# One decoder block on one core: token rows added in single steps between the last two experts' own operations, float32 spread of the last results, one root chain

## The chip, the cores and the metric

The kernel runs on one core of one Trainium2 chip. The metric is device time in microseconds (us) of one execution. A core has five engines with queues of their own that run in order and wait for each other through semaphores: PE (TensorE, matmuls; PEld is its weight loads), DVE (VectorE), ACT (ScalarE), POOL (GpSimd) and SP (SyncE, which here only issues DMAs).

## The reference, cut to what matters

512 tokens of width 1024. A token mixer comes first, then a mixture of 16 experts (4 groups of 4) of which each token takes two of one group, then a last norm.

```python
h = h + gate_m * _hybrid_mixer(...)
xf = _rms_norm(h, norm_ffn_w[l]) * (1.0 + scale_f) + shift_f
# in _hierarchical_moe, for each group gi:
    hg = jnp.einsum('td,edf->tef', xf, w_gate[gi])
    hu = jnp.einsum('td,edf->tef', xf, w_up[gi])
    act = jax.nn.silu(hg) * hu * comb[:, gi, :, None]
    out = out + jnp.einsum('tef,efd->td', act, w_down[gi])
h = h + gate_f * _hierarchical_moe(...)
return _rms_norm(h, norm_out_w)
```

## The kernel before

The kernel gathers each expert's tokens into a block of 128 rows, so that each of the 16 experts costs one pass of gate and up (`gate_up`: two sums of 24 matmuls of 128x512), SiLU and multiplication (L1497 on ACT, L1498 on DVE), transposes of the hidden rows with their split into a rounded and a residual part (`h_prep`, L1503 to L1506), and down (`down`: two halves `q` of 12 matmuls). Matmuls run on fp32r operands; float32 precision comes from three passes over a high and a low part (`PASSES`).

Experts 0 to 13 write their rows, by token and choice, to a DRAM buffer `yg`. The last two (14 and 15, `e >= NY`) don't: their results, times a weight per slot (`wsl`) and the gate row, are evicted to `ys` (L1520) and spread to the tokens by matmuls with a 0/1 selector `selT` (`spread_parts` makes the two parts, `spread_rows` issues the matmuls).

Meanwhile the rows of `yg` are read back, one DMA for each of the four token tiles t (`y_rows`), and added to the residual stream `hbs[t]` with each token's weights `comb` and the gate row (`add_rows`: a scaling on ACT, then three steps of 128x1024: one multiply-add on DVE, a multiplication and an addition on DVE, for tile 3 on POOL). At the end each half tile gets the spread sum from PSUM (L1754), is squared and summed on ACT (L1756), and for tiles 0 and 1 multiplied by the output norm's weights on POOL (L1758). `root` makes 1/rms for two tiles by a chain of 13 tiny DVE instructions (L1749, then `rsqrt`, L171 to L179), and the tiles are scaled (L1765 on ACT, L1767 on DVE) and stored (L1768).

The engines run what the program issues in its order. `after(j)` is called between the parts of `gate_up` and issues work of other kinds there; what it issues stands in the queues of ACT and DVE ahead of the SiLU and of L1498, since these are issued after the last matmul of `gate_up`.

Of the kernel before, what the change touches and what calls it, by code (L numbers as in the profile page):

```python
# [10 lines left out]
F32 = mybir.dt.float32  # L11
FR = mybir.dt.float32r
I32 = mybir.dt.int32
AF = mybir.ActivationFunctionType
ALU = mybir.AluOpType
# [4 lines left out]
D = 1024  # L20
S = 512
NT = S // P
# [4 lines left out]
EPS = 1e-6  # L27
# [87 lines left out]
def body(ctx, tc, x, c, mod_w, mod_b, norm_mix_w, w_in, gdn_conv_w, gdn_a_log, gdn_dt_bias, gdn_norm_w, w_out,  # L115
         norm_ffn_w, w_group, b_group, w_router, b_router, w_gate, w_up, w_down, norm_out_w, c_sq, c_ret, c_rt, out):
    nc = tc.nc
    act, dve, pe, pool, sp = nc.scalar, nc.vector, nc.tensor, nc.gpsimd, nc.sync
# [24 lines left out]
    rl_free, hi_free, lo_free = [], [], []  # L143
# [108 lines left out]
    def flat(t, n):  # L252
        return t.rearrange("p (k n) -> p k n", n=n)
# [44 lines left out]
    def two(key, n):  # L298
        return [flat(t, n) for t in parts[key]]
# [737 lines left out]
    for b, (kind, c0) in enumerate(wblocks):  # L1037
# [3 lines left out]
        if kind == "G":  # L1041
            pt = ps_m.tile([P, 512], F32, tag="m", name="pm")
            for k in range(KB):
                for i, (w, a) in enumerate(PASSES):
                    pe.matmul(pt[:8], lhsT=ws[w][:, k, :8], rhs=xs[a][k // 4][:, k % 4],
                              start=(k == 0 and i == 0), stop=(k == KB - 1 and i == 2))
# [109 lines left out]
    comb = cp.tile([P, NT, 2], F32, name="comb")  # L1156
# [147 lines left out]
    for t in range(NT):  # L1304
        py = [pst("py") for _ in range(2)]
        for q in range(4):
            w2 = two(("o", q), 256)
            for k in range(KB):
                for i, (a, w) in enumerate(PASSES):
                    pe.matmul(py[q // 2][:, (q % 2) * 256:(q % 2 + 1) * 256], lhsT=mhl[t][a][:, k], rhs=w2[w][:, k],  # L1310
                              start=(k == 0 and i == 0), stop=(k == KB - 1 and i == 2))
# [151 lines left out]
    def halves(t):  # L1463
        return t[:, 0:4], t[:, 4:8]
# [35 lines left out]
    def h_prep(hh, al=fresh):  # L1500
        th, tl, pt = al("th"), al("tl"), al("ht")
        for k in range(4):
            pe.transpose(out=pt[:, k * P:(k + 1) * P], in_=hh[:, k * P:(k + 1) * P], identity=ident)  # L1503
        p3 = pt.rearrange("p (k q) -> p k q", k=4)
        act.copy(out=th, in_=p3)  # L1505
        dve.tensor_tensor(out=tl, in0=p3, in1=th.bitcast(F32), op=ALU.subtract)  # L1506
        return th, tl

    def down(e, tt, q, o, al=fresh, wt=None):
        pt = al(f"py{q}")  # L1510
        hi_lo = two((e, 4 + q), 512)
        for k in range(4):
            for i, (a, w) in enumerate(PASSES):
                pe.matmul(pt, lhsT=tt[a][:, k], rhs=hi_lo[w][:, k],  # L1514
                          start=(k == 0 and i == 0), stop=(k == 3 and i == 2))
        if e == "ov" or e < NY:
            return lambda: act.copy(out=o, in_=pt)
        g = flat(loaded["g", 0], D)[:, 0, q * 512:(q + 1) * 512]
        if wt is not None:
            return lambda: dve.scalar_tensor_tensor(out=o, in0=pt, scalar=wt, in1=g, op0=ALU.mult, op1=ALU.mult)  # L1520
        return lambda: dve.tensor_tensor(out=o, in0=pt, in1=g, op=ALU.mult)
# [79 lines left out]
    tts, yb, spread, hbs = {}, {}, {}, {}  # L1601
# [12 lines left out]
        act.copy(out=selT[j], in_=pt.rearrange("p (t q) -> p t q", t=NT))  # L1614
        dve.tensor_copy(out=wsl[:, j:j + 1], in_=pw[:, :1])

    def spread_parts(j, ys, qq=(0, 1)):

        t = spread[j] if j in spread else flat(hi_free.pop(0), D)
        for q in qq:  # L1620
            qs = slice(q * 512, (q + 1) * 512)
            act.copy(out=t[:, 0, qs], in_=ys[:, qs])
            dve.tensor_tensor(out=t[:, 1, qs], in0=ys[:, qs], in1=t[:, 0, qs].bitcast(F32), op=ALU.subtract)
        spread[j] = t

    def spread_rows(j, t, q, pt):
        for a in range(2):
            pe.matmul(pt, lhsT=selT[j][:, t], rhs=spread[j][:, a, q * 512:(q + 1) * 512],
                      start=(j == 0 and a == 0), stop=(j == 1 and a == 1))

    def y_rows(t):

        if not rl_free:
            more_raw(slot_of[id(hi_free.pop(0))])
        yb[t] = flat(rl_free.pop(0), D)
        sp.dma_start(out=yb[t], in_=yg[2 * t * P:2 * (t + 1) * P].rearrange("(p i) d -> p i d", i=2))

    def add_rows(t):

        y0, y1 = (yb[t][:, i] for i in range(2))  # L1640
        act.activation(out=y0, in_=y0, func=AF.Copy, scale=comb[:, t, 0:1])
        dve.scalar_tensor_tensor(out=y0, in0=y1, scalar=comb[:, t, 1:2], in1=y0, op0=ALU.mult, op1=ALU.add)
        eng = pool if t == 3 else dve
        eng.tensor_tensor(out=y0, in0=y0, in1=gn[:, 0], op=ALU.mult)  # L1644
        eng.tensor_tensor(out=hbs[t], in0=hbs[t], in1=y0, op=ALU.add)  # L1645


    selT = []
    ws_gen = []
    for e in range(NE):  # L1650
        last = e == NE - 1
        hh = fresh("hh")

        def after(j, e=e):
            release((e, j))
            if j < (3 if e != EC else 0):
                split_next()
            for _ in range(2):
                if ws_gen and next(ws_gen[0], "end") == "end":
                    ws_gen.pop(0)  # L1660
            if e == 0 and j == 0:
                slot_rows()
                x_load(toks[:, 8:9], X)
            if e == 1 and j == 0:
                more_blocks()
            if e == NE - 1 and j < 2:
                last_slots(j)
            if e == NE - 1 and j >= 2:
                y_rows(j - 1)
                add_rows(j - 2)  # L1670
        if e == 0:
            xx1 = x_first(1)
            split_next(2)
        if last:
            assert pos[0] == len(seq)
            gn = flat(loaded["g", 0], D)
            for i in range(2):
                for j in range(2):
                    hbs[2 * i + j] = flat(loaded["t", i], D)[:, j]
            y_rows(0)  # L1680
        reserve[0] = 4 if e == EC - 1 else 0
        gate_up(e, xx, hh, after)
        if e == EC:
            more()
            split_next(4)
        elif not last:
            split_next()
        if e == NY:
            for j in range(2):
                for t in range(NT):  # L1690
                    dve.tensor_scalar(out=slot_sel(j)[:, t], in0=iota, scalar1=posa[:, t, NY + j:NY + j + 1],  # L1691
                                      scalar2=M[:, t, NY + j:NY + j + 1], op0=ALU.is_equal, op1=ALU.mult)
        if e == 0:
            xx = xx1
        elif not last:
            xx = x_prep(X)
            if e + 2 < NE:
                x_load(toks[:, (e + 2) * 4:(e + 2) * 4 + 1], X)
            if e == 1:
                rl_free.append(em.tile([P, 2048], F32, tag="rawl", name="rawl"))  # L1700
                load()
        if e:
            ys = fresh("ys")
            w = wsl[:, e - 1 - NY:e - NY] if e - 1 >= NY else None
            down(e - 1, tts[e - 1], 0, ys[:, :512], wt=w)()
            release((e - 1, 4))
            if not last:
                split_next()
        tts[e] = h_prep(hh)
        if e == 2:  # L1710
            ws_gen += [w012, w3]
        if e:
            down(e - 1, tts[e - 1], 1, ys[:, 512:], wt=w)()
            release((e - 1, 5))
            if w is None:
                y_store(rows[:, (e - 1) * 4:(e - 1) * 4 + 1], ys)
            else:
                spread_parts(0, ys)
                y_rows(3)
            if not last:  # L1720
                split_next()
        if e == NY:
            selT += halves(em.tile([P, KB, P], FR, tag="X", name="selT"))


    e = NE - 1
    ys = fresh("ys")
    ev = [down(e, tts[e], q, ys[:, q * 512:(q + 1) * 512], wt=wsl[:, 1:2]) for q in range(2)]
    pf = {}
    tq = [(t, q) for t in range(NT) for q in range(2)]  # L1730
    add_rows(2)
    for t, q in tq[:6]:
        pf[t, q] = list(banks.values())[2 * t + q]
        spread_rows(0, t, q, pf[t, q])
    for q in range(2):
        ev[q]()
        spread_parts(1, ys, (q,))
    add_rows(3)
    for t, q in tq:
        if t == NT - 1:  # L1740
            pf[t, q] = ps_m.tile([P, 512], F32, tag="m", name="pf")
            spread_rows(0, t, q, pf[t, q])
        spread_rows(1, t, q, pf[t, q])
    fs = em.tile([P, 2 * NT], F32, name="fs")
    fr = em.tile([P, NT], F32, name="fr")
    def root(t0):
        f2 = fs[:, 2 * t0:2 * t0 + 4].rearrange("p (t q) -> p t q", q=2)
        r2 = fr[:, t0:t0 + 2]
        dve.tensor_tensor(out=r2, in0=f2[:, :, 0], in1=f2[:, :, 1], op=ALU.add)  # L1749
        rsqrt(r2, r2, 1.0 / D, EPS)  # L1750

    for t, q in tq:
        h = hbs[t][:, q * 512:(q + 1) * 512]
        dve.tensor_tensor(out=h, in0=h, in1=pf[t, q], op=ALU.add)  # L1754
        j = em.tile([P, 512], F32, tag="hh", name="junk", bufs=2)
        act.activation(out=j, in_=h, func=AF.Square, accum_out=fs[:, 2 * t + q:2 * t + q + 1])  # L1756
        if t < 2:
            pool.tensor_tensor(out=h, in0=h, in1=gn[:, 1, q * 512:(q + 1) * 512], op=ALU.mult)  # L1758
        if (t, q) == (NT - 1, 0):
            root(0)  # L1760
    root(2)
    for t in range(NT):
        h = hbs[t]
        if t < 2:
# [33 lines left out]
```

## Time and profile before

| | us |
|---|---|
| median of 3 runs | 1088.85 |
| lowest, highest | 1085.78, 1088.94 |
| profiled execution, its own time | 1089.13 |
| its span (first to last instruction) | 1087.3 |

| engine | busy us | share of the span |
|---|---|---|
| PE | 963.2 | 89% |
| PE weight load | 835.7 | 77% |
| DVE | 736.0 | 68% |
| ACT | 518.0 | 48% |
| POOL | 295.7 | 27% |

The mean granted TensorE clock is 0.94 of 2.4 GHz. The shares are means over the whole span; the change touches only its last 65 us or so. Times in the rows below are counted from the start of the span.

### The profile page before, as it was taken

Reading aid. Unit: us, or ns where it says so; the run is one execution under the profiler, and the core shown is the slowest. Engines: PE = TensorE matmul, PEld = TensorE weight load, DVE = VectorE, ACT = ScalarE, POOL = GpSimd, SP = SyncE. Lnnn points to the kernel's source line nnn. Section 1 sums busy time; section 2 is a strip of 40 time slices with the busy share of each in tenths; the row PEclk is TensorE's granted clock in tenths of the full one; section 3 lists DMA queues with packets and bytes.
Section 4 is the critical chain, followed back from the end, with each engine's and each line's share of the span. In section 5 each row is a group of like instructions: output and inputs, shape, how many; then the busy total and the mean of one; then the engine's idle time right before and its main releaser. Section 6 shows DMA issues by size and latency. Waiting matters only on the chain. (4 is left out here: it accounts for less than half of the span.)

```text
span 1087.3 us, 14839 instructions
## 1 busy us (share of the span) xinstructions
PE 963.2 (89%) x5672; PEld 835.7 (77%) x5672; DVE 736.0 (68%) x1167; ACT 518.0 (48%) x750; POOL 295.7 (27%) x281
## 2 busy tenths in 40 slices
PE   4899989989889999999999977599967899999972
PEld 2579957768799999999989975478846688888851
DVE  3478246767886652566448594699766789898966
ACT  4453134433342331362233333478655778888823
POOL 2018733553447645000000154111100111111103
PEclk8999998989989989999999988799988999999987
DMA  9857742232345532232157245789784799999941
GB/s 297 268 177 249 222 138 83 83 113 82 128 136 145 165 117 79 69 107 79 40 161 252 98 154 75 283 322 388 245 307 171 287 389 384 376 383 365 358 164 78
DMA packets 139538, 217.91 MB, mean 200 GB/s; under 512 B 14942, under 2 KB 72830, under 8 KB 138692
## 3 DMA queue, kind: packets, MB, share of 16 engines
q1 hardware_dynamic: 124640, 182.45, 48.9%
q0 software_dynamic: 11296, 30.66, 9.1%
q10 hardware_dynamic: 3524, 3.78, 1.0%
q8 instruction: 47, 0.77, 0.3%
q14 instruction: 31, 0.25, 0.1%
HBM read 204.98 MB, written 21.16 MB: 208 GB/s over the span
## 5 line engine op out<-in xcount | busy, mean ns | idle before, releaser
L294 DVE TENSOR_TENSOR lo<-raw,hi 128x1024 fp32r<-128x1024 f32 (+1 forms) x194 | 242.0, 1287 | 57.9 <-ACT hi L293 57.8
L293 ACT CAST hi<-raw 128x1024 fp32r<-128x1024 f32 (+1 forms) x198 | 197.4, 1043 | 28.1 <-PE gu L1492 21.6
L1064 PE MATMUL pm<-lo,xh 128*128 128x256 f32 x640 | 186.5, 291 | 11.5 <-DVE ty L650 7.1
L1064 PE MATMUL pm<-hi,xh 128*128 128x256 f32 x640 | 186.5, 291 | 0.0
L1064 PE MATMUL pm<-hi,xl 128*128 128x256 f32 x640 | 185.9, 290 | 0.0
L1064 PEld LDWEIGHTS pm<-lo,xh 128*128 128x128 f32 x640 | 125.8, 196 | 12.4 <-issue 7.2
L1064 PEld LDWEIGHTS pm<-hi,xh 128*128 128x128 f32 x640 | 125.9, 197 | 0.5
L1064 PEld LDWEIGHTS pm<-hi,xl 128*128 128x128 f32 x640 | 125.8, 197 | 0.3
L1492 PE MATMUL gu<-lo,xth 128*128 128x512 f32 x256 | 103.7, 405 | 10.7 <-DVE lo L1559 9.2
L1492 PE MATMUL gu<-hi,xtl 128*128 128x512 f32 x256 | 103.1, 403 | 2.0 <-DVE xtl L1460 2.0
L1492 PE MATMUL gu<-hi,xth 128*128 128x512 f32 x256 | 103.1, 403 | 0.0
L393 POOL TENSOR_TENSOR rawm<-rawm 128x512 f32<-128x512 f32 (+2 forms) x96 | 100.3, 1044 | 7.7
L493 POOL DMA_DIRECT2D rawm<-in_mod_w_dram x32 | 29.7, 927 | 213.8 <-PE modp L510 202.3
L1064 PE MATMUL pm<-xl,hi 128*128 128x512 f32 x168 | 70.1, 417 | 2.0 <-ACT hi L293 1.6
L1064 PE MATMUL pm<-xh,lo 128*128 128x512 f32 x168 | 71.1, 423 | 0.5 <-DVE lo L294 0.5
L1064 PE MATMUL pm<-xh,hi 128*128 128x512 f32 x168 | 70.9, 422 | 0.0
L1492 PEld LDWEIGHTS gu<-lo,xth 128*128 128x128 f32 x256 | 49.4, 193 | 23.4 <-DVE lo L1559 9.6
L1008 ACT ACTIVATE sg<-pm 128x512 f32<-128x512 f32 x32 | 18.9, 597 | 95.9 <-PE pm L1064 81.1
L1514 PE MATMUL py<-lo,th 128*128 128x512 f32 x144 | 61.8, 429 | 1.4 <-ACT th L1505 1.4
L391 POOL TENSOR_TENSOR rawm<-rawm,cs 128x1024 f32<-128x1024 f32 x32 | 61.4, 1918 | 0.6
L1451 POOL DMA_INDIRECT X<-xfd,toks x14 | 20.3, 1448 | 148.8 <-PE xe L1472 128.8
L1492 PEld LDWEIGHTS gu<-hi,xtl 128*128 128x128 f32 x256 | 49.2, 192 | 14.3 <-DVE xtl L1460 2.4
(405 smaller groups left out, 2037.0 us busy)
## 6 DMA issues: line engine op xcount, KB each, us to landing
raw<-in_w_in_dram SPq DMA_DIRECT2D x32, 1024.0 KB
raw<-in_w_up_dram SPq DMA_DIRECT2D x26, 1024.0 KB
raw<-in_w_gate_dram SPq DMA_DIRECT2D x24, 1024.0 KB
raw<-in_w_down_dram SPq DMA_DIRECT2D x20, 1024.0 KB
rawm<-in_mod_w_dram POOLq DMA_DIRECT2D x32, 512.0 KB, 5.2
rawe<-in_w_down_dram SPq DMA_DIRECT2D x9, 1024.0 KB
rawe<-in_w_up_dram SPq DMA_DIRECT2D x8, 1024.0 KB
mod<-in_mod_w_dram SPq DMA_DIRECT2D x7, 1024.0 KB
```

What stands on the lines that cost most here:

```text
L293: act.copy(out=hi, in_=rw)
L294: (eng or dve).tensor_tensor(out=lo, in0=rw, in1=hi.bitcast(F32), op=ALU.subtract)
L391: pool.tensor_tensor(out=r, in0=r, in1=cs.unsqueeze(2).to_broadcast([P, KB, n]), op=ALU.mult)
L393: pool.tensor_tensor(out=r[:, :m], in0=r[:, :m], in1=r[:, m:2 * m], op=ALU.add)
L493: pool.dma_start(out=r, in_=mw[:, :, (16 + i) * P:(17 + i) * P])
L1008: act.activation(out=sg, in_=pt, func=AF.Sigmoid)
L1064: pe.matmul(o, lhsT=l, rhs=r, start=st, stop=sp__)
L1451: pool.indirect_dma_start(out=X, out_offset=None, in_=xfd, in_offset=bass.IndirectOffsetOnAxis(ap=at, axis=0), bounds_check=S - 1, oob_is_ ...
L1492: pe.matmul(pt, lhsT=xx[a][k // 4][:, k % 4], rhs=hi_lo[w][:, k % 4], start=(k == 0 and i == 0), stop=(k == KB - 1 and i == 2))
L1514: pe.matmul(pt, lhsT=tt[a][:, k], rhs=hi_lo[w][:, k], start=(k == 0 and i == 0), stop=(k == 3 and i == 2))
```

## The change

Four edits, all at the end of the program.

1. `add_rows` becomes a generator that yields after each of its three DVE steps, all tiles' on DVE; its scaling on ACT is a function of its own (`scale_rows`). Nothing of it is issued inside `gate_up` any more. Tile 0's steps are issued one or two at a time between the operations of experts 14 and 15, tile 1's after expert 14's spread parts, tiles 2 and 3's after expert 15's evictions.
2. Tile 3's multiplication and addition move from POOL to DVE.
3. Expert 15's results are spread by one float32 matmul from `ys` for each tile and half (L1762 of the changed program), in place of two fp32r matmuls of its two parts, which are no longer made.
4. One root chain for all four tiles stands behind the last addition, in place of one for tiles 0 and 1 (ahead of the last addition) and one for 2 and 3.

```diff
-    def spread_parts(j, ys, qq=(0, 1)):
+    def spread_parts(j, ys):
...
+    def scale_rows(t):
+        y0 = yb[t][:, 0]
+        act.activation(out=y0, in_=y0, func=AF.Copy, scale=comb[:, t, 0:1])
+
     def add_rows(t):
 
         y0, y1 = (yb[t][:, i] for i in range(2))
-        act.activation(out=y0, in_=y0, func=AF.Copy, scale=comb[:, t, 0:1])
         dve.scalar_tensor_tensor(out=y0, in0=y1, scalar=comb[:, t, 1:2], in1=y0, op0=ALU.mult, op1=ALU.add)
-        eng = pool if t == 3 else dve
-        eng.tensor_tensor(out=y0, in0=y0, in1=gn[:, 0], op=ALU.mult)
-        eng.tensor_tensor(out=hbs[t], in0=hbs[t], in1=y0, op=ALU.add)
+        yield
+        dve.tensor_tensor(out=y0, in0=y0, in1=gn[:, 0], op=ALU.mult)
+        yield
+        dve.tensor_tensor(out=hbs[t], in0=hbs[t], in1=y0, op=ALU.add)
+        yield
+
+    def all_rows(ts):
+        for t in ts:
+            yield from add_rows(t)
...
                 y_rows(j - 1)
-                add_rows(j - 2)
...
-            down(e - 1, tts[e - 1], 0, ys[:, :512], wt=w)()
+            ev = down(e - 1, tts[e - 1], 0, ys[:, :512], wt=w)
+            if last:
+                scale_rows(0)
+                adds = all_rows(range(NT))
+                next(adds)
+                next(adds)
+            ev()
...
         tts[e] = h_prep(hh)
+        if last:
+            next(adds)
...
                 spread_parts(0, ys)
                 y_rows(3)
+                for t in range(1, NT):
+                    scale_rows(t)
+                for _ in range(3):
+                    next(adds)
...
-    add_rows(2)
     for t, q in tq[:6]:
         pf[t, q] = list(banks.values())[2 * t + q]
         spread_rows(0, t, q, pf[t, q])
     for q in range(2):
         ev[q]()
-        spread_parts(1, ys, (q,))
-    add_rows(3)
+    for _ in adds:
+        pass
     for t, q in tq:
...
-        spread_rows(1, t, q, pf[t, q])
+        pe.matmul(pf[t, q], lhsT=selT[1][:, t].bitcast(F32), rhs=ys[:, q * 512:(q + 1) * 512], start=False, stop=True)
...
-        if (t, q) == (NT - 1, 0):
-            root(0)
-    root(2)
+    f2 = fs.rearrange("p (t q) -> p t q", q=2)
+    dve.tensor_tensor(out=fr, in0=f2[:, :, 0], in1=f2[:, :, 1], op=ALU.add)
+    rsqrt(fr, fr, 1.0 / D, EPS)
```

What the diff alone doesn't tell is the order on the engines. DVE, behind the last copy of the slot weights (`wsl`), as it was (`raw_88`, `rawe_5906` hold the rows of tiles 0 and 1, `raw_4775` the residual stream of both):

```order
L1615 COPY wsl<-py_9060 128x1
L1642 SCALAR_TENSOR_TENSOR raw_88<-raw_88,comb 128x1024
L1644 TENSOR_TENSOR raw_88<-raw_88,raw_89 128x1024
L1645 TENSOR_TENSOR raw_4775<-raw_4775,raw_88 128x1024
L1642 SCALAR_TENSOR_TENSOR rawe_5906<-rawe_5906,comb 128x1024
L1644 TENSOR_TENSOR rawe_5906<-rawe_5906,raw_89 128x1024
L1645 TENSOR_TENSOR raw_4775<-raw_4775,rawe_5906 128x1024
L1498 TENSOR_TENSOR hh<-hh,gu_5885 128x512
L1520 SCALAR_TENSOR_TENSOR ys<-py_9108,wsl,raw_89 128x512
L1506 TENSOR_TENSOR tl<-xe,th 128x512
```

And now, from the same place to the second eviction of the last expert:

```order
L1498 TENSOR_TENSOR hh<-hh,gu_5885 128x512
L1645 SCALAR_TENSOR_TENSOR raw_88<-raw_88,comb 128x1024
L1647 TENSOR_TENSOR raw_88<-raw_88,raw_89 128x1024
L1520 SCALAR_TENSOR_TENSOR ys<-py_9100,wsl,raw_89 128x512
L1506 TENSOR_TENSOR tl<-xe,th 128x512
L1649 TENSOR_TENSOR raw_4775<-raw_4775,raw_88 128x1024
L1520 SCALAR_TENSOR_TENSOR ys<-py_9126,wsl,raw_89 128x512
L1623 TENSOR_TENSOR hi_5459<-ys,hi_5459 128x512 x2
L1645 SCALAR_TENSOR_TENSOR rawe_5906<-rawe_5906,comb 128x1024
L1647 TENSOR_TENSOR rawe_5906<-rawe_5906,raw_89 128x1024
L1649 TENSOR_TENSOR raw_4775<-raw_4775,rawe_5906 128x1024
L1520 SCALAR_TENSOR_TENSOR ys<-py_9152,wsl,raw_89 128x512
```

L1498 has moved ahead of all adding steps; tile 0's steps (L1645, L1647, L1649) stand apart, around the eviction and `tl`.

ACT, behind the second selector cast (`selT`) and up to the squares, as it was:

```order
L1614 CAST selT<-xe 128x512
L1641 ACTIVATE raw_88<-raw_88,comb 128x1024
L1641 ACTIVATE rawe_5906<-rawe_5906,comb 128x1024
L1497 ACTIVATE hh<-gu_5884 128x512
L1505 CAST th<-xe 128x512
L1622 CAST hi_5459<-ys 128x512 x2
L1641 ACTIVATE rawe_5907<-rawe_5907,comb 128x1024
L1622 CAST hi_92<-ys 128x512 x2
L1641 ACTIVATE raw_5037<-raw_5037,comb 128x1024
```

And now:

```order
L1614 CAST selT<-xe 128x512
L1497 ACTIVATE hh<-gu_5884 128x512
L1640 ACTIVATE raw_88<-raw_88,comb 128x1024
L1505 CAST th<-xe 128x512
L1622 CAST hi_5459<-ys 128x512 x2
L1640 ACTIVATE rawe_5906<-rawe_5906,comb 128x1024
L1640 ACTIVATE rawe_5907<-rawe_5907,comb 128x1024
L1640 ACTIVATE raw_5037<-raw_5037,comb 128x1024
```

The SiLU (L1497) has moved ahead of the scalings, the other three scalings stand together, and two casts are gone.

PE, the difference behind the last expert's down (`hi_5459` holds expert 14's parts, `hi_92` held expert 15's):

```order
 L1628 MATMUL xe<-hi_5459,selT 128x512 x8
-L1628 MATMUL gu_5884<-hi_92,selT 128x512 x2
-L1628 MATMUL gu_5885<-hi_92,selT 128x512 x2
-L1628 MATMUL xe<-hi_92,selT 128x512 x8
+L1762 MATMUL gu_5884<-ys,selT 128x512
+L1762 MATMUL gu_5885<-ys,selT 128x512
+L1762 MATMUL xe<-ys,selT 128x512 x4
 L1628 MATMUL pf<-hi_5459,selT 128x512 x2
-L1628 MATMUL pf<-hi_92,selT 128x512 x2
+L1762 MATMUL pf<-ys,selT 128x512
```

One float32 matmul stands where two fp32r ones stood.

## Rows read from the trace of the kernel before

**Rows 1.** Who waited for whom, 1034 to the end: total us, times, longest.

```profile
PE xe L1503 <- DVE hh L1498: 8.1, 1, 8.1
```

**Rows 2.** Order of time (ACT, PE, DVE): start, us, instruction, [idle before, releaser].

```profile
1031.88 0.58 ACT L1614 CAST selT<-xe 128x512 fp32r<-128x512 f32 x1
...
1039.35 1.15 ACT L1641 ACTIVATE raw<-raw,comb 128x1024 f32<-128x1024 f32 x1 [6.88 <-DMA raw<-yg]
...
1040.23 0.39 PE L1514 MATMUL py<-hi,tl 128*128 128x512 f32 x1
1040.54 1.28 DVE L1642 SCALAR_TENSOR_TENSOR raw<-raw,comb 128x1024 f32<-128x1024 f32 x1 [6.48 <-ACT raw L1641]
...
1042.89 0.58 ACT L1497 ACTIVATE hh<-gu 128x512 f32<-128x512 f32 x1
...
1047.97 0.68 DVE L1498 TENSOR_TENSOR hh<-hh,gu 128x512 f32<-128x512 f32 x1
1048.57 0.74 DVE L1520 SCALAR_TENSOR_TENSOR ys<-py,wsl,raw 128x512 f32<-128x512 f32 x1
```

**Rows 3.** By stretch: length, busy (count) of five engines, clock, DMA share, GB/s.

```profile
1044.00:1052.00 8.00, 3.29 (x11) 2.83 (x12) 5.93 (x7) 1.10 (x2) 0.00 (x0) 0.57 0.17 70
...
22.30:24.30 2.00, 1.98 (x3) 0.50 (x3) 0.00 (x0) 0.00 (x0) 0.00 (x0) 0.50 1.09 341
```

**Rows 4.** Order of time, PE: matmuls behind the hole, and of the spread.

```profile
1050.05 0.63 PE L1514 MATMUL py<-hi,th 128*128 128x512 f32 x1
...
1050.47 0.63 PE L1514 MATMUL py<-hi,tl 128*128 128x512 f32 x1
...
1059.85 2.03 PE L1628 MATMUL xe<-hi,selT 128*128 128x512 f32 x8
```

**Rows 5.** Order of time, POOL and DVE, from 1065 to the last multiplications.

```profile
1065.63 2.41 POOL L1644 TENSOR_TENSOR raw<-raw,raw 128x1024 f32<-128x1024 f32 x1 [38.26 <-DVE raw L1642]
...
1070.43 4.93 POOL L1758 TENSOR_TENSOR raw<-raw,raw 128x512 f32<-128x512 f32 x4
1070.50 0.69 DVE L1754 TENSOR_TENSOR raw<-raw,pf 128x512 f32<-128x512 f32 x1 [1.37 <-POOL raw L1645]
1071.11 0.60 DVE L1749 TENSOR_TENSOR fr<-fs 128x2 f32<-128x2 f32 x1
...
1071.75 1.20 DVE L171 TENSOR_SCALAR nx<-fr 128x2 f32<-128x2 f32 x1
...
1077.06 0.68 DVE L1754 TENSOR_TENSOR raw<-raw,pf 128x512 f32<-128x512 f32 x1
...
1078.59 0.16 DVE L1749 TENSOR_TENSOR fr<-fs 128x2 f32<-128x2 f32 x1 [0.85 <-ACT junk L1756]
...
1081.16 2.48 DVE L1767 SCALAR_TENSOR_TENSOR raw<-raw,fr,raw 128x1024 f32<-128x1024 f32 x2
```

**Rows 6.** Order of time, DVE and ACT: spread parts, then half-tile additions.

```profile
1054.19 1.46 DVE L1623 TENSOR_TENSOR hi<-ys,hi 128x512 fp32r<-128x512 f32 x2
...
1060.51 0.62 ACT L1622 CAST hi<-ys 128x512 fp32r<-128x512 f32 x1 [4.53 <-DVE ys L1520]
...
1066.66 2.48 DVE L1754 TENSOR_TENSOR raw<-raw,xe 128x512 f32<-128x512 f32 x4
```

**Rows 7.** Order of time, PE, early: float32 matmuls of 128x512 (two instructions each).

```profile
22.32 2.05 PE L336 MATMUL rrow<-diag,ones 128*128 128x512 f32 x2 [6.80 <-DVE diag L334]
...
258.59 1.02 PE L570 MATMUL rs<-rqk 128*128 128x512 f32 x2
...
259.68 0.39 PE L1064 MATMUL pm<-xl,hi 128*128 128x512 f32 x1
```

**Rows 8.** Order of time, ACT and SP's queue: last scalings, first store.

```profile
1078.46 2.17 ACT L1765 ACTIVATE raw<-raw,fr 128x1024 f32<-128x1024 f32 x2
...
1079.62 4.38 SPq L1768 DMA_DIRECT2D out_dram<-raw  x4
```

**Rows 9.** By stretch, columns as in rows 3: the stores.

```profile
1080.40:1085.90 5.50, 0.00 (x0) 0.00 (x0) 3.10 (x6) 0.23 (x1) 0.00 (x0) 0.50 0.96 381
```

More of the change, by code (lines that the diff above doesn't have):

```diff
@@ L1615, in last_slots @@
         dve.tensor_copy(out=wsl[:, j:j + 1], in_=pw[:, :1])
-    def spread_parts(j, ys, qq=(0, 1)):
-        t = spread[j] if j in spread else flat(hi_free.pop(0), D)
-        for q in qq:
+    def spread_parts(j, ys):
+        t = flat(hi_free.pop(0), D)
+        for q in range(2):
             qs = slice(q * 512, (q + 1) * 512)
@@ L1628, in spread_rows @@
             pe.matmul(pt, lhsT=selT[j][:, t], rhs=spread[j][:, a, q * 512:(q + 1) * 512],
-                      start=(j == 0 and a == 0), stop=(j == 1 and a == 1))
+                      start=(a == 0), stop=False)
     def y_rows(t):
@@ L1742, in body @@
             spread_rows(0, t, q, pf[t, q])
-        spread_rows(1, t, q, pf[t, q])
+        pe.matmul(pf[t, q], lhsT=selT[1][:, t].bitcast(F32), rhs=ys[:, q * 512:(q + 1) * 512], start=False, stop=True)
     fs = em.tile([P, 2 * NT], F32, name="fs")
     fr = em.tile([P, NT], F32, name="fr")
[L1746 to L1750, printed above, removed]
     for t, q in tq:
```

## Prediction

> **What bounds the kernel now.** The front of the kernel isn't touched, so I read only the end: from the last expert's gate and up products, at about 1024 us, to the end of the span at 1087.3. I began with the waits of this stretch, then the order of time on ACT, DVE and PE, then the chain that ended last.
>
> The longest wait on PE is 8.1 us: the transposes of the last expert's hidden rows wait for the multiplication `hh` on DVE [rows 1]. The order of time says why [rows 2]. ACT ends its selector cast at 1032.46 and then stands in the scaling of token tile 0's rows until 1039.35, when those rows land. The SiLU is queued behind that scaling and tile 1's and runs at 1042.89, although its gate sums were done before the selector cast. DVE does the six adding steps of tiles 0 and 1 from 1040.54 to 1047.97 and only then `hh`. PE's last matmul before the hole starts at 1040.23. Behind the hole its granted clock averages 0.57 over 1044 to 1052, that is 1.2 GHz for most of it [rows 3], and matmuls start 0.42 us apart [rows 4], where 0.234 is the distance at 2.4 GHz (eight in 2.03 us, the last 0.39 long).
>
> The second hole is on DVE at the very end. POOL does two of tile 3's steps from 1065.63, both about 2.4 us, and its four weight multiplications wait until 1070.43. DVE stands until 1070.50 for tile 3's sum, adds one half tile, and then does the first root chain while POOL multiplies: its first instruction takes 0.60 us instead of 0.16, the next three 1.20 each instead of 0.17 (the second chain, 13 instructions from 1078.59 to 1081.16, shows the undisturbed size). The last half tile is added only at 1077.06, the second chain lasts to 1081.16, and two multiplications (2.48) and the stores end the span [rows 5].
>
> **The change, step by step.** I lay DVE's new queue out from 1040.54, the start of tile 0's first adding step. That start stays: it hangs on rows landing at 1039.35 plus a scaling, and neither their issue nor what is ahead of it moves. What changes ahead of it: the SiLU now follows the selector cast (about 1032.5) and `hh` follows the last up matmul. PE issues 12 matmuls between the last up matmul and 1040.23 + 0.234, so `hh` runs near 1038 and is done when PE comes to the transposes at 1040.5. The hole of 8.1 us goes, and with it the half clock.
>
> Prices from the rows: a tile's three steps take 7.43/2 = 3.72 us, an eviction 0.74, a residual 0.73 (two in 1.46), the hi cast on ACT 0.62, a scaling 1.15 [rows 2, 6].
> - Tile 0's steps one and two end at 1043.1. First half of the eviction to 1043.8, the residual `tl` of the hidden rows to 1044.5, step three (1.2) to 1045.7, second half evicted at 1046.45, its hi cast on ACT to 1047.1, its residual to 1047.85.
> - ACT's scaling of tile 1 stands behind that cast: to 1048.3. This costs DVE 0.4 us, the only wait that I find on it. Tile 1's steps to 1052.0, the last expert's two evictions to 1053.5.
> - Tiles 2 and 3, both now on DVE: 7.43, to 1060.9. The moved part is POOL's two passes of 2.4 us, which cost DVE 2.4 in all; what goes against it are two casts, two residuals (1.46) and the handing to and fro between them.
> - Eight half-tile additions, 0.6 apart (four in 2.48, the last 0.68 long) [rows 5, 6]: the last starts at 1060.9 + 7 x 0.6 = 1065.1. Before, it started at 1077.06, so 12 us have gone by here.
>
> PE beside this: after the transposes (to about 1040.9) twelve matmuls to 1043.9, then the last expert's 24. The third of them needs `tl` (1044.5), so they end near 1050. Twelve spread matmuls end at 1052.5 and the eight float32 ones start with the first evicted half at 1052.8. For their price the trace has one case at the full clock: a 128x512 float32 matmul is two instructions, and from its start to the next but one matmul lie 259.68 - 258.59 = 1.09 us, less 0.234 for the matmul between: 0.86 [rows 7]. The other end is 2.05 us, early in the kernel at a granted clock of 0.50 [rows 3, 7]. I take 0.86, since PE has no hole ahead of it. Eight of them and the four remaining spread matmuls are 6.9 + 0.9, to 1060.6, and each is there before DVE asks for it; the last with 4.5 us to spare. That cover hides the 3.1 us that eight at 0.86 cost over the sixteen at 0.234 removed; it is gone from 0.86 + 4.5/8 = 1.4 us each, and from there each 0.1 us more costs 0.8.
>
> The one root chain starts 1.53 us after the last addition (1077.06 to 1078.59, with the square between): 1066.6. POOL's first multiplication follows the first addition and its square, some 1.4 us, so 1062.3, and four take 4.93: to 1067.2. So the chain's first instruction meets the fourth multiplication and waits for its end, 0.6 us; the rest runs free, 2.4 us (the whole chain took 2.57), to 1069.65. In the rows of before one DVE instruction ended with each POOL instruction, which is how I price this. The Trainium skill (SBUF — State Buffer, section "SBUF: two separate sides") states such a rule: DVE and POOL share a pair of ports that one of them holds for a whole instruction, while the other blocks. It speaks against a single chain placed behind POOL's work, and the 1.20 us rows agree with it; by the rule as by the row it costs 0.6 here, or more if POOL is later (a rival below).
>
> Now the stores. Tiles 0 and 1 used to be scaled and stored while the second chain ran: first store issued at 1079.62. Now all four wait for one chain. The first is ready after a scaling of 1.13 (two took 2.17, overlapping a little) at 1070.8, the others by 1072.2 [rows 8]. In before 2.10 MB moved in the 5.5 us from 1080.4 at a DMA share of 0.96, beginning 0.8 after the first issue, and the span ended 1.4 later [rows 9]. At a share of one that is 5.3: 1070.8 + 0.8 + 5.3 + 1.4 = 1078.3. By the other bound, the last multiplication, it would be 1072.15 plus the 3.66 that lay between its end and the span's end before (1083.64 to 1087.3): 1075.8. I take the later, since the transfers kept nearly all the DMA busy.
>
> **The sum.** 1087.3 - 1078.3 = 9.0 us less. The profiled execution took 1089.13, 1.83 over its span and 0.28 over the median of 1088.85. So 1080.1 against that execution, and 1079.9 by the median. The first hole gives back about 8, the second about 4 more with the root; the queue of stores takes some 2.5 of it.
>
> **Rivals.**
> - Stores don't bind, because the DMA engines take the four together faster than one by one: 1075.8 + 1.83 - 0.28 = 1077.3. For it: some of the 5.5 us were gaps between issues. Against: the share of 0.96. Chance 0.12.
> - POOL holds the whole head of the chain as before, if its multiplications start about 3 us later than I have them. The first chain of before, 1071.11 to 1077.0, was 5.9 against 2.57, so 3.4 more instead of my 0.6: 1079.9 + 2.8 = 1082.7. For it: exactly these rows. Against: POOL has nothing else in its queue now. Chance 0.12.
> - No change: the rows of tile 0 now stand on DVE ahead of `tl` and of both evictions, so each us that they land after 1039.35 moves PE and everything behind by one. From 5.7 us late on, what is left is within 3.3 us (0.3%) of before, about what a measurement can tell. For it: DVE takes its instructions in order, and the landing already ended ACT's 6.88 us wait. Against: nothing ahead of these transfers changes. Chance 0.05.
> - Slower: PE stays at the half clock from the transposes on, and the float32 matmuls take the 2.05 of that row. Then 36 matmuls at 0.42 end at 1056.7, the twelve spread ones at 1061.8, and 8 x 2.05 + 4 x 0.42 end at 1079.9. With 1.53, the chain's 2.57, 1.13 and 7.5 for the stores the span is 1092.6, the time 1094.1. At the full clock it would take 3.0 us for each float32 matmul to become slower by 0.3%. For it: the half clock was there in this very stretch. Against: the hole that came before it is gone, and the granted clock was back at 2.4 GHz, by the 0.234, once PE worked again. Chance 0.03.
> - The rest, 0.02, I leave to sides that I don't see.
>
> **The numbers.** The forecast has 0.66, with a range of its own of 1078.5 to 1082: the handovers between ACT and DVE may each cost some tenths more, and the runs of before lie 3 us apart. The range given reaches to both neighbours, 1075.5 to 1084, and leaves out the two far cases. Faster by over 0.3%: forecast and both neighbours, 0.90; within 0.3%: 0.06; slower: 0.04.
>
> **What would show it.** `hh` near 1038 and no wait of PE's transposes for it; PE's clock at 1.00 until the float32 matmuls end; these 0.86 us apart, done near 1061; no POOL instruction before the multiplications; the first half-tile addition near 1061 and eight without a gap; the root's first instruction stretched, the others at 0.17; the four stores issued within 1.5 us and the DMA full behind them. I am wrong if DVE waits anywhere for PE between 1048 and 1065, if tile 0's rows land later, or if the chain's head shows 1.2 us instructions again.

## The result and the profile after

The changed kernel takes 1076.32 us (median of 4 runs, 1073.98 to 1081.39) against 1088.89 (4 runs, 1085.78 to 1089.45): a ratio of 0.9897, 95% interval 0.9855 to 0.9938. It is faster, by 11.2 us of the 1088.89, between 6.8 and 15.8 (the medians alone lie 12.6 apart). Its profiled execution took 1077.67, with a span of 1075.9.

The end of the program is compared best from one instruction that every version has: the first adding step of tile 0 on DVE (1040.54 before, 1038.45 after). From it to the end of the span I call "the stretch" below: 46.8 us before, 37.45 after, 9.3 less.

PE's wait for `hh` [rows 1] is gone. These are the waits of 1034 to 1080 after (engine, instruction, releaser: total us, times, longest). POOL and ACT stand long for work that isn't due yet; DVE, whose queue sets this stretch, has waits of 4.6 and 0.8 ahead of its first step, of 0.4 and 0.9 behind it, and no more:

```profile
ACT raw L1640 <- DMA raw<-yg: 5.2, 1, 5.2
DVE hh L1498 <- PE gu L1492: 4.6, 1, 4.6
...
DVE fr L1773 <- ACT junk L1769: 0.9, 1, 0.9
DVE raw L1645 <- ACT raw L1640: 0.8, 1, 0.8
...
DVE rawe L1645 <- ACT rawe L1640: 0.4, 1, 0.4
```

The order of time after (start, us, instruction, [idle before, releaser]), the part that answers to [rows 2], [rows 5] and [rows 8]:

```profile
1037.01 0.69 DVE L1498 TENSOR_TENSOR hh<-hh,gu 128x512 f32<-128x512 f32 x1 [4.62 <-PE gu L1492]
...
1037.26 1.15 ACT L1640 ACTIVATE raw<-raw,comb 128x1024 f32<-128x1024 f32 x1 [5.22 <-DMA raw<-yg]
...
1038.45 1.28 DVE L1645 SCALAR_TENSOR_TENSOR raw<-raw,comb 128x1024 f32<-128x1024 f32 x1 [0.76 <-ACT raw L1640]
...
1039.54 0.60 PE L1503 MATMUL xe<-sq,hh 128*128 128x128 f32 x4
...
1045.78 1.28 DVE L1645 SCALAR_TENSOR_TENSOR rawe<-rawe,comb 128x1024 f32<-128x1024 f32 x1 [0.36 <-ACT rawe L1640]
...
1049.50 1.40 DVE L1520 SCALAR_TENSOR_TENSOR ys<-py,wsl,raw 128x512 f32<-128x512 f32 x2
1050.82 1.27 DVE L1645 SCALAR_TENSOR_TENSOR rawe<-rawe,comb 128x1024 f32<-128x1024 f32 x1
1051.18 1.88 PE L1762 MATMUL gu<-ys,selT 128*128 128x512 f32 x4
...
1052.89 3.60 PE L1762 MATMUL xe<-ys,selT 128*128 128x512 f32 x8
...
1058.12 1.02 PE L1762 MATMUL pf<-ys,selT 128*128 128x512 f32 x2
1058.25 1.27 DVE L1767 TENSOR_TENSOR raw<-raw,gu 128x512 f32<-128x512 f32 x2
...
1059.44 2.47 DVE L1767 TENSOR_TENSOR raw<-raw,xe 128x512 f32<-128x512 f32 x4
...
1059.77 4.96 POOL L1771 TENSOR_TENSOR raw<-raw,raw 128x512 f32<-128x512 f32 x4 [34.23 <-ACT junk L1769]
...
1061.83 1.27 DVE L1767 TENSOR_TENSOR raw<-raw,pf 128x512 f32<-128x512 f32 x2
...
1064.03 0.71 DVE L1773 TENSOR_TENSOR fr<-fs 128x4 f32<-128x4 f32 x1 [0.93 <-ACT junk L1769]
1064.78 0.17 DVE L171 TENSOR_SCALAR nx<-fr 128x4 f32<-128x4 f32 x1
...
1067.16 2.48 DVE L1780 SCALAR_TENSOR_TENSOR raw<-raw,fr,raw 128x1024 f32<-128x1024 f32 x2
1067.22 2.19 ACT L1778 ACTIVATE raw<-raw,fr 128x1024 f32<-128x1024 f32 x2 [3.22 <-DVE fr L179]
1068.39 2.93 SPq L1781 DMA_DIRECT2D out_dram<-raw  x4
```

`hh` runs as soon as PE's last up matmul is there, and the transposes (1039.54) follow without a wait. The eight half-tile additions go without a gap from 1058.25, the single root chain begins at 1064.03, and only its first instruction is stretched (0.71), as POOL's fourth multiplication ends at 1064.73 (1059.77 + 4.96).

By stretch (columns as in [rows 3]), after:

```profile
1044.00:1052.00 8.00, 8.00 (x34) 6.12 (x33) 7.48 (x9) 3.75 (x4) 0.00 (x0) 1.00 0.01 2
1052.00:1060.00 8.00, 7.14 (x19) 3.23 (x17) 7.86 (x9) 1.04 (x3) 0.23 (x1) 1.00 0.00 0
1069.20:1074.50 5.30, 0.00 (x0) 0.00 (x0) 0.44 (x1) 0.20 (x1) 0.00 (x0) 0.50 1.00 396
```

PE is busy in all 8 us of 1044 to 1052, where it had 3.29 [rows 3], and its granted clock is 1.00 (2.4 GHz) there and while the float32 matmuls run. DVE is busy 15.3 of 16 us. In the last row the stores fill the DMA engines (share 1.00), as they nearly did before [rows 9].

### The profile page after: what moved, and what is told of

Same layout as the page of the kernel before. It is cut to its first block, busy times and chain, and to the rows that moved or that the text cites. A ratio compares the mean times of both kernels' runs of the same rounds, so it can differ in the third digit from the quotient of the medians.

```text
span 1075.9 us, 14821 instructions
## 1 busy us (share of the span) xinstructions
PE 961.5 (89%) x5672; PEld 831.5 (77%) x5672; DVE 734.1 (68%) x1154; ACT 516.6 (48%) x748; POOL 290.7 (27%) x279
## 5 line engine op out<-in xcount | busy, mean ns | idle before, releaser
L1492 PE MATMUL gu<-lo,xth 128*128 128x512 f32 x256 | 104.3, 408 | 11.2 <-DVE lo L1559 9.6
```

The costliest lines, as they stand in the source:

```text
L1492: pe.matmul(pt, lhsT=xx[a][k // 4][:, k % 4], rhs=hi_lo[w][:, k % 4], start=(k == 0 and i == 0), stop=(k == KB - 1 and i == 2))
```

## The experiments

The theory: DVE's queue from the adding step on is the bound, with the stores behind it, and each edit is worth what it takes out of that queue or out of waits in it. The main rivals: that the hole on PE with its half clock was all of the gain, or that one of the other edits was no gain, or a loss hidden by the rest. "Stretch" is measured in each kernel's profile; the ratios are to the kernel before on the same chip.

| kernel | stretch | median us | ratio, 95% interval |
|---|---|---|---|
| before | 46.8 | 1088.89 | |
| before, again (e5) | 47.3 | 1086.53 | 0.999, 0.997 to 1.001 |
| changed | 37.45 | 1076.32 | 0.9897, 0.9855 to 0.9938 |
| changed, again (e6) | 37.4 | 1075.68 | 0.9895, 0.9861 to 0.9928 |
| changed, third (e9) | 37.4 | 1077.54 | 0.9918, 0.989 to 0.9946 |
| e1, order undone | 44.4 | 1084.05 | 0.9973, 0.9953 to 0.9992 |
| e2, tile 3 on POOL | 37.9 | 1078.37 | 0.9925, 0.9907 to 0.9942 |
| e3, two rounded parts | 40.2 | 1079.46 | 0.9927, 0.9904 to 0.9951 |
| e4, two root chains | 38.7 | 1078.57 | 0.9929, 0.9909 to 0.9949 |
| e7, order alone | 42.0 | 1083.96 | 0.9963, 0.9943 to 0.9984 |
| e8, e2 and no weights on POOL | 35.3 | 1078.45 | 0.992, 0.9893 to 0.9947 |
| e10, e8 again | 35.4 | 1073.92 | 0.9883, 0.985 to 0.9917 |
| e11, no weights on POOL | 37.5 | 1077.49 | 0.9898, 0.9866 to 0.993 |
| e12, float32 matmuls doubled | 39.8 | 1079.29 | 0.9936, 0.9909 to 0.9964 |

The stretch repeats to 0.1 us where a kernel ran again after the change (37.45, 37.4, 37.4; 35.3, 35.4) and to 0.5 before it. The medians spread by 2 us and more for one kernel, so what follows is read from the stretch, and the ratios are beside it.

**e1: the order undone.** Tiles 0 and 1 are scaled and added inside `gate_up` again; the rest stays changed.

```diff
                 y_rows(j - 1)
+                scale_rows(j - 2)
+                for _ in add_rows(j - 2):
+                    pass
...
-                scale_rows(0)
-                adds = all_rows(range(NT))
-                next(adds)
-                next(adds)
+                adds = all_rows(range(2, NT))
...
```

> The changed kernel with its order undone alone: tiles 0 and 1 are added inside the last gate and up again, ahead of the SiLU and of hh; all else as changed. Theory (the hole on PE feeds the whole tail): the hole of about 8 us on PE and the half clock come back, the last expert's evictions wait for PE near 1057, and from tile 0's first adding step to the end of the span it takes 44 to 46 us instead of 37.5 (time some 7 us more than the changed kernel). Rival (DVE's sum of work sets the end and the order of it doesn't matter): 37.5 to 39.

The stretch is 44.4, 6.9 longer than after. The hole is back; first the waits of e1, then its order of time, then 1044 to 1052 by stretch:

```profile
PE xe L1503 <- DVE hh L1498: 7.8, 1, 7.8
DVE ys L1520 <- PE py L1514: 5.1, 3, 2.4
```

```profile
1045.46 0.68 DVE L1498 TENSOR_TENSOR hh<-hh,gu 128x512 f32<-128x512 f32 x1
```

```profile
1044.00:1052.00 8.00, 5.80 (x21) 4.83 (x22) 4.38 (x7) 1.24 (x3) 0.00 (x0) 0.67 0.01 2
```

PE stands 7.8 us for `hh`, the clock is down again, and DVE waits 5.1 us in three places for the sums that PE brings later. The 0.67 is a mean over another part of the stretch than that of before: 1044 lies 6.0 us behind tile 0's first step here (1038.03) and 3.5 behind it in [rows 3]. From 3.5 on (1041.5 to 1049.5) e1 has PE busy for 3.30 us at a mean clock of 0.57, which is the picture of before. Without the order, 2.4 of the 9.3 us are left.

**e2: tile 3's two steps on POOL, as before.**

```diff
+        eng = pool if t == 3 else dve
-        dve.tensor_tensor(out=y0, in0=y0, in1=gn[:, 0], op=ALU.mult)
+        eng.tensor_tensor(out=y0, in0=y0, in1=gn[:, 0], op=ALU.mult)
...
```

> The changed kernel with tile 3's multiplication and addition back on POOL. Theory: in the new order this is no longer a price, since six half-tile additions cover most of POOL's 4.8 us; the last addition starts about 1 us earlier, but POOL's four multiplications end 0.9 later and stretch three instructions of the root chain: 37.5 to 38.5 from tile 0's first step to the end (changed: 37.5). Rival (POOL's passes were the second hole and their move is the gain there): 41 or more.

0.45 longer. DVE, in the order of time of e2, waits for POOL and then has the head of the root chain stretched:

```profile
1060.80 1.28 DVE L1768 TENSOR_TENSOR raw<-raw,pf 128x512 f32<-128x512 f32 x2 [1.34 <-POOL raw L1650]
...
1062.95 0.28 DVE L1774 TENSOR_TENSOR fr<-fs 128x4 f32<-128x4 f32 x1 [0.87 <-ACT junk L1770]
1063.27 1.19 DVE L171 TENSOR_SCALAR nx<-fr 128x4 f32<-128x4 f32 x1
1064.49 1.19 DVE L172 TENSOR_SCALAR na<-nx 128x4 int32<-128x4 int32 x1
```

The 2.4 us that DVE saves are eaten by a wait of 1.34 and by two instructions at 1.19 for 0.17, as POOL's multiplications now start later. Edit 2 pays only half a microsecond, by keeping POOL out of the chain.

**e3: two rounded parts of expert 15's results, as before.**

```diff
...
         ev[q]()
+        spread_parts(1, ys, (q,))
...
-        pe.matmul(pf[t, q], lhsT=selT[1][:, t].bitcast(F32), rhs=ys[:, q * 512:(q + 1) * 512], start=False, stop=True)
+        spread_rows(1, t, q, pf[t, q])
```

> The changed kernel with the last expert's results spread in two rounded parts again (16 fp32r matmuls, two casts, two residuals). Theory: DVE is the bound, so two residuals and two handovers from ACT cost 2.7 us: about 40.2 from tile 0's first step to the end. Rival (the float32 matmuls' 3.1 us on PE are not hidden): as fast as the changed kernel or faster, 34.5 to 37.5.

40.2, 2.7 longer: two residuals on DVE, some 0.6 each, and two waits of 0.68 for the casts, one of which is this, from the order of time of e3:

```profile
1050.43 0.69 DVE L1623 TENSOR_TENSOR hi<-ys,hi 128x512 fp32r<-128x512 f32 x1 [0.68 <-ACT hi L1622]
```

**e4: two root chains, as before.**

```diff
...
+        if (t, q) == (NT - 1, 0):
+            root(0)
+    root(2)
-    dve.tensor_tensor(out=fr, in0=f2[:, :, 0], in1=f2[:, :, 1], op=ALU.add)
-    rsqrt(fr, fr, 1.0 / D, EPS)
```

> The changed kernel with two root chains again, the first ahead of the last half-tile addition. Theory: the first chain meets the last two or three of POOL's multiplications (two instructions stretched to about 1.2 us), the last addition starts near 4.5 us later, and stores that start earlier give most of it back: 38 to 39.5 from tile 0's first step to the end. Rival (the queue of four stores costs more than a second chain): 35.5 to 37.2.

1.3 longer. The first chain stands in the middle of POOL's multiplications, and the last addition waits behind it to 1064.99; the order of time of e4:

```profile
1060.59 1.09 DVE L1768 TENSOR_TENSOR fr<-fs 128x2 f32<-128x2 f32 x1
1061.71 1.19 DVE L171 TENSOR_SCALAR nx<-fr 128x2 f32<-128x2 f32 x1
...
1064.99 0.68 DVE L1773 TENSOR_TENSOR raw<-raw,pf 128x512 f32<-128x512 f32 x1
```

**e5, e6, e9: both kernels unchanged,** to see how well stretch and time repeat.

> The kernel before once more, unchanged. Both theories expect a ratio of 1 and, from tile 0's first adding step to the end, the 46.8 us of the first profile. It tells whether that step's start (1040.5 in the first profile of before, 1036.6 to 1038.5 in the five profiles of changed programs) belongs to the program (again 1040 or later) or to the single execution (anywhere from 1036 to 1041).

> The changed kernel once more, unchanged. From tile 0's first adding step to the end 37.5 us again; if what went beyond the 9.3 us of this stretch is chance of the single executions, the ratio lies at 0.991 to 0.992 rather than 0.990.

> The changed kernel a third time, unchanged, beside the next three on the same chip: 37.4 us from tile 0's first adding step to the end, as in its two profiles. It is the measure for the next two.

Their numbers stand in the table. The stretch came as expected (47.3, and 37.4 twice), and in e5 its first step starts at 1037.90, so where it starts belongs to the single execution. The ratio of e6, 0.9895, isn't the 0.991 to 0.992 that I had expected; e9's, 0.9918, is. All three intervals of the changed kernel hold the 9.3 us of the stretch, so the times don't show that the change gives more than that.

**e7: the order alone,** that is, the edits of e2, e3 and e4 together.

> The kernel before with the new order alone: single steps between the last experts' operations, but tile 3 on POOL, two rounded parts and two root chains. Theory: 41.8 us from tile 0's first step to the end (before 46.8): closing PE's hole gives 8, but POOL's two passes end behind six half-tile additions, and its four multiplications then stretch the head of the first chain as before. Rival (the four edits simply add up: 2.7 + 1.3 + 0.5 = 4.5 over the changed kernel): 42.0, which is no different; the third theory, that the hole on PE is all of the change: 37.5 to 39.

42.0, so the order alone gives 4.8 us of 46.8 (5.3 of e5's 47.3), and the other three edits 4.5 more, which is the sum of what undoing each alone costs (0.45 + 2.7 + 1.3). That the hole was all is refuted. In e7 PE has no hole and DVE no wait for PE's sums, yet DVE still waits for POOL and both casts. Its order of time, to be laid beside [rows 5]:

```profile
1054.66 0.69 DVE L1623 TENSOR_TENSOR hi<-ys,hi 128x512 fp32r<-128x512 f32 x1 [0.68 <-ACT hi L1622]
...
1065.23 0.69 DVE L1775 TENSOR_TENSOR raw<-raw,pf 128x512 f32<-128x512 f32 x1 [1.38 <-POOL raw L1650]
1065.84 0.60 DVE L1770 TENSOR_TENSOR fr<-fs 128x2 f32<-128x2 f32 x1
1066.47 1.20 DVE L171 TENSOR_SCALAR nx<-fr 128x2 f32<-128x2 f32 x1
```

**e8 and e10: a version that goes further.** Tile 3's steps on POOL as in e2, no weight multiplications on POOL (DVE scales and weights all four tiles in one instruction each), and tile 1's scaling on ACT ahead of the second cast.

```diff
...
         tts[e] = h_prep(hh)
         if last:
             next(adds)
+            scale_rows(1)
...
-        if t < 2:
-            pool.tensor_tensor(out=h, in0=h, in1=gn[:, 1, q * 512:(q + 1) * 512], op=ALU.mult)
...
-        if t < 2:
-            act.activation(out=h, in_=h, func=AF.Copy, scale=fr[:, t:t + 1])
-        else:
-            dve.scalar_tensor_tensor(out=h, in0=h, scalar=fr[:, t:t + 1], in1=gn[:, 1], op0=ALU.mult, op1=ALU.mult)
+        dve.scalar_tensor_tensor(out=h, in0=h, scalar=fr[:, t:t + 1], in1=gn[:, 1], op0=ALU.mult, op1=ALU.mult)
```

> The changed kernel with tile 3's two passes on POOL, no weight multiplications on POOL (all four tiles get weights and root in one DVE step each), and tile 1's scaling on ACT ahead of the second half's cast. Theory: DVE's 0.4 us wait goes, the last addition starts about 1.3 earlier, no instruction of the chain is stretched, and four stores follow each other every 1.25 us: 35.3 from tile 0's first step to the end, 2.1 less than the changed kernel. Rival (the stores' 5.3 us bind from their first issue, which two ACT scalings gave as early): 36.5 to 37.5.

> The kernel of e8 once more. Its stretch was 35.3 us, 2.1 less than the changed kernel's, but its time was 2 to 3 us more, with 7 us lost ahead of the stretch in the profiled execution. If that loss is chance of single executions (in its profile the granted clock fell to 0.74 near 390 us, where no instruction differs), it is now 0 to 4 us faster than the changed kernel beside it; if the loss belongs to this program, it is slower again.

The stretch is 35.3 and 35.4, 2.1 under the changed kernel's, and the places show it in e10: no wait of tile 1's first step, and a chain that starts undisturbed.

```profile
1043.62 1.28 DVE L1645 SCALAR_TENSOR_TENSOR rawe<-rawe,comb 128x1024 f32<-128x1024 f32 x1
...
1060.72 0.16 DVE L1773 TENSOR_TENSOR fr<-fs 128x4 f32<-128x4 f32 x1 [0.86 <-ACT junk L1771]
...
1063.31 4.87 DVE L1777 SCALAR_TENSOR_TENSOR raw<-raw,fr,raw 128x1024 f32<-128x1024 f32 x4
```

The times don't settle it. In e8's comparison it was 2.8 us over e6 by the medians, in e10's it was 3.6 us under e9, with intervals that overlap both times. Over all executions its median is 1076.6 (12) against 1077.5 (17). The gain in the stretch is shown, a gain in the time isn't.

**e11: the weights off POOL alone** (the last two hunks of e8).

> The changed kernel without POOL's four weight multiplications alone (all four tiles get weights and root in one DVE step each after the chain). Theory: the chain's first instruction is no longer stretched (0.16 in place of 0.71), and stores issued 1.25 apart keep the DMA full: 36.9 us from tile 0's first step to the end. Rival (the later second to fourth store lengthen the end): 38 or more.

37.5, as if nothing had changed, which neither side expected. The chain's first instruction does take 0.16, and the first store is issued 0.4 earlier in the stretch (1069.53 - 1040.03 = 29.5, against 29.9). The data of the stores end earlier too, 35.5 us into the stretch (at about 1075.5) against 36.0 (1074.4). What the edit gave is lost behind the data: from their end to that of the span it takes 1.9 us in place of 1.4. In the closing instructions of the program SP waits 1.0 us for PE's queue, and 0.5 in each of the other 13 profiles. These waits of e11 and then of after:

```profile
SPq L1801 <- PEq L1801: 1.2, 2, 1.0
```

```profile
SPq L1806 <- PEq L1806: 0.7, 2, 0.5
```

e8 and e10, whose stores are issued in the same way, have the 0.5. Whether the longer closing is chance or belongs to this program, one profile doesn't tell.

**e12: each float32 matmul issued twice,** to find PE's cover.

```diff
-        pe.matmul(pf[t, q], lhsT=selT[1][:, t].bitcast(F32), rhs=ys[:, q * 512:(q + 1) * 512], start=False, stop=True)
+        for a in range(2):
+            pe.matmul(pf[t, q], lhsT=selT[1][:, t].bitcast(F32), rhs=ys[:, q * 512:(q + 1) * 512], start=False, stop=a == 1)
```

> The changed kernel with each of the eight float32 matmuls issued twice (the last expert's rows are counted twice). It puts 6.9 us more on PE, ahead of the last half-tile additions. By the cover of the prediction (about 3.3 us from PE's last float32 matmul to the last addition in the profile after), 3.6 us more on the last addition, less the 0.55 of the chain's stretched instruction, which POOL then misses: 40.5 us from tile 0's first step to the end. Rival (PE has no part in the end, or the price per matmul isn't 0.86): 37.4, or 42 and more.

39.8, 2.35 longer, less than expected. DVE waits for PE at the last two additions, in e12's order of time:

```profile
1058.47 0.69 DVE L1768 TENSOR_TENSOR raw<-raw,pf 128x512 f32<-128x512 f32 x1 [1.25 <-PE pf L1763]
...
1060.65 0.69 DVE L1768 TENSOR_TENSOR raw<-raw,pf 128x512 f32<-128x512 f32 x1 [1.50 <-PE pf L1763]
```

The last addition starts 2.9 later in the stretch than after (1060.65 - 1033.74 = 26.9, against 24.0). So 6.9 us more on PE (8 x 0.86) cost 2.9, and 4.0 were covered, 0.7 more than the 3.3 that I had taken from the profile after. In e12 PE was that much further ahead of DVE to begin with: its float32 matmuls start 12.05 us into the stretch (1045.79), where after they start 12.73 into it (1051.18).

```profile
1045.79 3.60 PE L1763 MATMUL gu<-ys,selT 128*128 128x512 f32 x8
```

Tile 0's first step waits for a DMA, so PE's place against it differs from one execution to the next: the last up matmul starts between 1.7 and 3.5 us ahead of it in the 14 profiles. Without those 0.7 the stretch would have been 40.4, the 40.5 that was expected. Half a microsecond comes back because the chain's first instruction is no longer stretched.

## Why the prediction was right, point by point

1079.9 was forecast and 1076.32 measured. That is below the 1078.5 to 1082 which the forecast gave itself, and nearer to the 1077.3 of the rival in which the stores don't bind: by the time alone the rival did better. It is the trace that shows the likeliest case, and in it the main size was nearly right: the profiled span was forecast at 1078.3 and is 1075.9. Of these 2.4 us, 2.1 lie ahead of the stretch and 0.3 in it; the rest, some 1.1, is that the median of after lies 1.35 under its profiled execution, and that of before only 0.28. Counted from tile 0's first adding step:

| step | forecast | after |
|---|---|---|
| first half-tile addition | 20.4 | 19.8 |
| start of the last addition | 24.6 | 24.0 |
| start of the root chain | 26.1 | 25.6 |
| end of the chain | 29.1 | 28.7 |
| first store issued | 30.3 | 29.9 |
| end of the span | 37.8 | 37.45 |

- **DVE's queue.** The one wait that I found on it, 0.4 for tile 1's scaling, is there with 0.36. The 20 us to the additions were forecast 0.6 too long, since I added lengths where the next instruction starts a little ahead of the end: from the last two evictions to the step behind them lie 1.32 (1049.50 to 1050.82), not 1.5.
- **Where the gain came from: mis-sized.** "The first hole gives back about 8, the second about 4 more with the root; the queue of stores takes some 2.5 of it" comes near the sum and has the wrong shares; the forecast itself, 9.0, was added up from DVE's queue and not from these shares. The order alone gave 4.8 to 5.3 and the other three edits 4.5. PE's hole of 8.1 wasn't idle time of the bound: DVE did adding steps in 7.4 us of it [rows 2], and those had to be done somewhere. What the order really takes from the stretch is `hh` itself (0.6, now ahead of it) and DVE's waits behind the hole; these are the waits of before, 1034 to the end:

```profile
DVE raw L1642 <- ACT raw L1641: 6.8, 2, 6.5
...
DVE ys L1520 <- PE py L1514: 2.4, 1, 2.4
...
DVE tl L1506 <- ACT th L1505: 1.2, 1, 1.2
```

  The 6.5 lies ahead of the stretch, the other 0.3 of that line in it. 0.6 + 2.4 + 1.2 + 0.3 is 4.5 of the 4.8. Undoing the order in e1 costs more, 6.9, because there tiles 2 and 3 are added behind the evictions and no longer fill part of these waits (5.1 us instead of 2.4). The half clock is a small part of what PE lost: from the transposes to the sixth matmul behind them it is 2.98 us before (1048.70 to 1051.68) and 1.60 after (1039.54 to 1041.14), so 1.4 us, against 8.1 of standing.
- **Float32 matmuls.** 0.86 forecast; two take 1.71 (1051.18 to 1052.89), 0.855 each, at the full clock. The last ends at 1059.14, 3.3 us ahead of the last addition at 1062.43 (the second of the pair at 1061.83, 0.6 behind the first); 4.5 was forecast. So the cover would be gone from 0.86 + 3.3/8 = 1.27 us each, against 1.4 in the prediction; in e12, where PE was 0.7 further ahead, from 0.86 + 4.0/8 = 1.36. The slower case fell with the clock of 1.00.
- **The chain beside POOL.** One instruction at 0.71 (0.76 forecast) and the others free. How many are stretched goes by when POOL's multiplications end: none without them (e8, e10, e11) or with a later chain (e12), one after, two to three in e2 (0.28, 1.19, 1.19), two in e4's first chain, four in e7's. This is the rule that the prediction drew on (the Trainium skill, SBUF — State Buffer, section "SBUF: two separate sides"), and these traces agree. The half-tile additions, with an operand in PSUM, run beside POOL's multiplications unstretched (four in 2.47).
- **The stores.** DMA share 1.00 over 5.3 us, and 1.4 from there to the end: the forecast. The rival in which they don't bind ends 3.66 after the last multiplication; it ended at 1069.64 and the span 6.3 later. From the first issue to the last it took 1.9 us and not the 1.5 forecast, which cost nothing, since the DMA engines were full: e8, e10 and e11 take 3.6 us for it, and their data end 6.0 us behind the first issue all the same.
- **What is ahead of the stretch.** The forecast kept its start at 1040.54. In the 14 profiles it lies between 1033.74 and 1043.96, for kernels that differ ahead of it only in the place of the last SiLU and `hh`. It differs as much for one kernel (before 1040.54 and 1037.90, e8's kernel 1043.96 and 1036.73) as between kernels, so I take these 2.1 us for spread between executions and not for the change; this is argued and not shown. The profile of before, from which the forecast took 1040.54, is one of the two that lost 4.7 us near 391 us (last section).

## What to carry to other kernels

A hole on one engine is worth what it costs the engine that sets the end. When that engine fills the hole with its own work, as DVE did with 7.4 of 8.1 us, closing it gives back only the waits behind it: lay out the bound engine's queue, step by step, and count its waits. A fixed instruction near the change makes a better ruler than the whole time: here it repeats to 0.1 us after the change (0.5 before it), where the medians of one kernel lie 2 us apart. But look at both of its ends: the closing in e11 and PE's head start in e12 moved it by 0.5 and 0.7 us. Long POOL work should end before a chain of tiny DVE instructions begins, since each of its instructions that meets POOL can cost 1.2 us instead of 0.17.

## What the runs showed that I had not expected

One part of the spread ahead of the stretch can be seen. Near 391 us, PE waits 2.2 us for `sg` on ACT, far ahead of anything that the change touches. In two of the 14 profiles (before and e8) the granted clock fell behind that wait; in e10 it fell in part (mean 0.93); in the other 11 it stayed at 1.00. PE in the order of time, and 388 to 412 by stretch, first before:

```profile
391.78 0.38 PE L1064 MATMUL pm<-lo,xh 128*128 128x256 f32 x1 [2.22 <-ACT sg L1008]
```

```profile
388.00:412.00 24.00, 21.78 (x148) 21.58 (x146) 11.70 (x22) 5.48 (x7) 6.99 (x7) 0.79 0.32 105
```

and then after:

```profile
392.64 0.39 PE L1064 MATMUL pm<-lo,xh 128*128 128x256 f32 x1 [2.21 <-ACT sg L1008]
```

```profile
388.00:412.00 24.00, 21.79 (x188) 21.58 (x186) 15.83 (x26) 5.48 (x7) 12.35 (x11) 1.00 0.43 132
```

The same wait, on the same instruction, is followed by a mean clock of 0.79 and 148 matmuls in the one case, and by 1.00 and 188 in the other. Counted in PE's order of time, the program's matmuls 2001 to 2400 take 53.4 us before (and in e8), 48.7 after: 4.7 us of spread in which the change has no part. What decides between the two is open.
